# Plain blocks for the first weight tile, and partial sums kept in PSUM, in the feed-forward stage of an encoder kernel on one Trainium2 core

## The chip, the cores and the metric

The kernel runs on one core of one Trainium2 chip. The time is the device time of one execution in microseconds (us); the median of three runs of the kernel before is 2502.7 us, with runs from 2497.94 to 2503.45 us. The engines are TensorE (PE, with its weight loads as PEld), VectorE (DVE), ScalarE (ACT), GpSimd (POOL) and SyncE (SP), whose queue issues all transfers between HBM and the on-chip memory. "Granted clock" is the share of full speed that TensorE was allowed.

## The reference, cut to what matters

Two requests of 1024 tokens, each 1024 wide, go through one encoder layer with shared weights. The part that matters here is the feed-forward network behind attention:

```python
FFN_HIDDEN = -(-8 * D_MODEL // (3 * 256)) * 256      # 2816
...
xn = rms_norm(h, norm_ffn_g[l])
g, u = jnp.split(xn @ w_gate_up[l], 2, axis=-1)
h = h + (jax.nn.silu(g) * u) @ w_down[l]
h = rms_norm(h, final_norm_g)
```

Everything is float32. The kernel splits each float32 operand into a high and a low part of a reduced type (fp32r) and forms one product from three matmuls (high by high, high by low, low by high; `mm3`).

## The kernel before

The program treats request 0 and then request 1; each passes projection, attention and feed-forward. The feed-forward stage is written for Strassen's method in Winograd's form: a 2 by 2 block product in seven block products instead of eight. The products are called P1 to P7, and their operands are blocks or sums of blocks.

**Gate and up.** The input of this stage, 1024 tokens by 1024, is cut into four blocks: B11 and B21 are the two halves of the width for the even tiles of 128 tokens, B12 and B22 those for the odd tiles. The seven products need B11, B21 and B22 and the sums T1 to T4 of blocks, each transposed. `x_side` is a generator that makes these 28 pieces (seven operands by four tiles): VectorE or GpSimd forms the sums from the normalised rows `x2n`, TensorE transposes 128 by 128 pieces (`x_trans`, four transposes into one PSUM bank, tile name `tp`), ScalarE copies the high part out, and VectorE takes the remainder as the low part (`xB`, `xT`, `xT1l`, `xH` in the profile; sums in tile `t`). It runs beside the end of attention's output projection, and the rest of it is stepped between the matmuls of the first two weight tiles. There are 22 weight tiles of 128 gate and 128 up columns. `gu_unit(p, t)` computes one product of one tile: 4 steps of depth with 3 matmuls of 512 columns each, 12 matmuls; 84 for a tile. `prep_gu` makes the weight operand of a product, up to six operand tiles ahead (`prep`, ring `wop`). The result of a tile (`act`) goes to HBM as `ad`.

**Down.** The activations are read back (`a_load`, blocks `A[i, j, c]`, i for even or odd tokens, j for even or odd weight tile, c from 0 to 10), and the residual `h` is read back from `hd`. A product has 11 blocks c of 12 matmuls, 132 in all, 924 for the seven. `DN` gives the order of the products: P1, P2, P4, P5, P7, P6, P3. Each product has its own four PSUM banks, and when it is complete VectorE adds its banks onto `h` once for every output block that contains it (`C`, `add`, list `adds`), spread over the matmuls of the next product: 14 output blocks by 4 banks, 56 additions for a request. `prep_dn` forms the sums of activations and of weight rows and makes the high parts, `prep_dn_lo` the low ones (VectorE for the weights, GpSimd for the activations). They run ahead of TensorE by at most three blocks. The rows of `w_down` come in two ways: `trun` holds the first 512 columns of the even rows for the whole stage, and `wraw` is a ring of four tiles, each loaded in the order of the list `items` when the tile four places earlier has been freed (`load`, set `freed`).

**The order on SyncE's queue.** All transfers are issued by SyncE in the order of the program text. Behind the last product of the last weight tile, `gu_hook` issues the burst of loads that the down stage needs: the rest of `trun`, the rest of the activations of the early products, `h` (8 transfers of 512 KB), and the activations A[2, 2] (`aC`, `aB`) and A[2, 1] (`aD`, `aB`, `aS`). The core of it:

```python
elif p == "P3":
    for c in (6, 8, 10):
        T.trun_tile(c)
    ...
    for t_ in range(TT):
        sync.dma_start(out=h[:, t_, :], in_=T.hd[:, t_, :])
    a_load(2, 2, 0, hold["C"], 0, 8)
```

The main loop calls, for unit n, first `T.prep_ops(n)` (which also makes the low parts up to unit n + 1 and calls `load`), then the matmuls of the unit, then `gu_hook`. The low part of block 1 of the first down product is made in the call for the first down unit, so behind the burst in the program text.

## Time and profile before

| what | us |
|---|---|
| median of three runs | 2502.7 |
| the profiled execution | 2502.41 |
| its span, first to last instruction | 2500.6 |
| TensorE busy in it | 2357.3 (94%) |
| VectorE busy in it | 1790.1 (72%) |
| GpSimd busy in it | 1262.2 (50%) |
| ScalarE busy in it | 1188.8 (48%) |

The span is 1.8 us shorter than the profiled time. Busy time of TensorE is modelled from the start of pipelined matmuls, so a stage in which matmuls start late one after another can still read as busy; the count of matmuls in a stretch of known length says more. All rows of the kernel read L118, since one helper records every operation; operations are told apart by their tiles.

### The profile page before, as it was taken

To read this page: it belongs to the slowest core of one execution; us is meant where nothing else is said; L and a number is where in the kernel's file an instruction comes from. 1 tells how busy PE (TensorE), PEld (TensorE's weight loads), DVE (VectorE), ACT (ScalarE), POOL (GpSimd) and SP (SyncE) were. 2 spreads that over 40 slices of the span, in tenths; PEclk is the share of its full clock that TensorE was granted. 3 is DMA by queue.
4 is the path that set the end of the run, shared out by engine and by line. 5 is a ranking of instruction groups with operands and counts; after the bars stand their busy time and mean duration, and the time that the engine had idled before them with its cause. 6 is when DMAs were issued, how large, how long until landed. Compare 5 with 4: busy or idle time off the path is not lost. (4 is left out here: it accounts for less than half of the span.)

```text
span 2500.6 us, 34045 instructions
## 1 busy us (share of the span) xinstructions
PE 2357.3 (94%) x12402; PEld 1992.9 (80%) x12402; DVE 1790.1 (72%) x2480; ACT 1188.8 (48%) x2131; POOL 1262.2 (50%) x1156
## 2 busy tenths in 40 slices
PE   7998999988999999999988989999799999999997
PEld 7887899877888888777777789988678888887765
DVE  6686888876555555599966778888765555556996
ACT  4476667654232222343545776666542223224434
POOL 5323766644444444465663157665444444444665
PEclk9999999998999999999999989999999999999999
DMA  5113000111223222842430130001122222237413
GB/s 140 39 36 103 18 18 18 43 68 43 85 77 92 76 77 93 328 151 76 144 129 22 36 103 26 10 18 43 68 68 76 76 85 83 86 123 298 168 48 114
DMA packets 189704, 212.78 MB, mean 85 GB/s; under 512 B 24272, under 2 KB 141008, under 8 KB 188512
## 3 DMA queue, kind: packets, MB, share of 16 engines
q1 hardware_dynamic: 189536, 210.60, 25.8%
q8 instruction: 98, 1.61, 0.3%
q14 instruction: 70, 0.57, 0.1%
HBM read 168.45 MB, written 39.85 MB: 83 GB/s over the span
## 5 line engine op out<-in xcount | busy, mean ns | idle before, releaser
L118 PE MATMUL dn<-wop 128*128 128x512 f32 x1848 | 449.6, 401 | 18.3 <-DVE wop L118 14.7
L118 PEld LDWEIGHTS dn<-wop 128*128 128x128 f32 x1848 | 343.5, 189 | 117.6 <-DVE wop L118 36.9
L118 PE MATMUL gu<-xT,wop 128*128 128x512 f32 x1408 | 371.3, 394 | 0.0
L118 POOL TENSOR_TENSOR pexp<-pexp,rsum 128x1024 f32<-128x1024 f32 x128 | 242.9, 1898 | 228.7 <-DVE rsum L118 148.5
L118 POOL TENSOR_TENSOR wop<-wraw,wop 128x512 fp32r<-128x512 f32 x176 | 230.6, 1311 | 217.5 <-ACT wop L118 217.5
L118 PEld LDWEIGHTS gu<-xT,wop 128*128 128x128 f32 x1408 | 264.2, 188 | 59.2
L118 POOL TENSOR_TENSOR wop<-wsum,wop 128x512 fp32r<-128x512 f32 x132 | 171.7, 1301 | 266.9 <-ACT wop L118 266.9
L118 PE MATMUL gu<-xB,wop 128*128 128x512 f32 x1056 | 265.1, 398 | 3.0 <-DVE xB L118 3.0
L118 ACT CAST wop<-wraw 128x512 fp32r<-128x512 f32 x264 | 162.6, 616 | 215.4 <-DVE wraw L118 134.2
L118 PE MATMUL gu<-xH,wop 128*128 128x512 f32 x1056 | 254.7, 397 | 1.7 <-DVE act L118 1.7
L118 PEld LDWEIGHTS gu<-xH,wop 128*128 128x128 f32 x1056 | 198.8, 188 | 50.3 <-issue 2.5
L118 PEld LDWEIGHTS gu<-xB,wop 128*128 128x128 f32 x1056 | 199.3, 190 | 48.8 <-DVE xB L118 3.6
L118 ACT CAST pt<-ptp 128x512 fp32r<-128x512 f32 x256 | 148.9, 586 | 120.1 <-PE ptp L118 118.9
L118 DVE TENSOR_REDUCE m<-S 128x1 f32<-128x1041 f32 x128 | 158.1, 1235 | 55.6 <-PE S L118 54.8
L118 ACT ACTIVATE pexp<-S,m 128x1041 f32<-128x1041 f32 x128 | 145.1, 1133 | 66.9 <-DVE m L118 60.0
L118 DVE TENSOR_TENSOR pt<-ptp,pt 128x512 fp32r<-128x512 f32 x256 | 168.2, 681 | 5.4 <-ACT pt L118 4.4
L118 PE MATMUL ptp<-idf,pexp 128*128 128x128 f32 x1024 | 156.4, 277 | 10.2 <-DVE pt L118 6.7
L118 PE MATMUL pvo<-pt,vst 128*128 128x256 f32 x1024 | 156.5, 297 | 2.9 <-DVE attnT L118 2.9
L118 PE MATMUL S<-kh,qs 128*128 128x348 f32 (+1 forms) x384 | 136.9, 359 | 21.3 <-ACT pexp L118 14.9
L118 ACT CAST wop<-wsum 128x512 fp32r<-128x512 f32 x132 | 81.8, 620 | 141.9 <-DVE wsum L118 141.9
L118 DVE SCALAR_TENSOR_TENSOR act<-th,act 128x512 f32<-128x512 f32 x88 | 143.7, 1633 | 3.0
L118 PEld LDWEIGHTS ptp<-idf,pexp 128*128 128x128 f32 x1024 | 125.9, 143 | 21.3 <-issue 7.8
(289 smaller groups left out, 5189.2 us busy)
## 6 DMA issues: line engine op xcount, KB each, us to landing
wraw<-in_w_gate_up SPq DMA_DIRECT2D x176, 256.0 KB, 3.6
wraw<-in_w_down SPq DMA_DIRECT2D x110, 256.0 KB, 2.9
ad<-act SPq DMA_DIRECT2D x44, 512.0 KB, 3.5
wraw<-in_w_down SPq DMA_DIRECT2D x22, 512.0 KB, 3.3
wraw<-in_w_in SPq DMA_DIRECT2D x32, 256.0 KB, 3.4
hd<-h SPq DMA_DIRECT2D x16, 512.0 KB, 5.0
h<-hd SPq DMA_DIRECT2D x16, 512.0 KB, 10.3
out<-h SPq DMA_DIRECT2D x15, 512.0 KB, 2.6
```

Of the source, the lines that this page charges most:

```text
L118: return fn(*args, **kw)
```

## The change

- **First weight tile of gate and up.** Tile 0 is no longer computed by the seven products but by the eight plain block products (`FIRST`, `gu_first`): four weight blocks, each against two token blocks, 96 matmuls, added up in four PSUM banks. The transposed blocks that it needs are B11, B12, B21, B22; B12 is a new operand of `x_side`. The sums T2, T3 and T4 and their transposes are made between the matmuls of tile 0, and T1 last, in the buffers that B12 had.
- **Order of the down products.** It becomes P2, P1, P4, P6, P5, P7, P3. P6 and P7 go on adding in the banks of P1, and P3 in those of P5 (`onto`), so that an output block is added to `h` from a bank that holds several products. 8 output blocks by 4 banks are left, 32 additions for a request.
- **Preparation of the down operands.** The sums of activations are others. P1 and P7 get weight rows of their own through the ring (`two("P1", 1, L0)`, `two("P7", 0, L0)`), 22 transfers of 256 KB more for a request, and the additions that alternated between VectorE and GpSimd are all on VectorE.
- **Loads.** A[1, 2] takes the places and the times of A[1, 1] and the other way round. The burst of `gu_hook` is otherwise the same.

```diff
 GU = (("P1", "B11"), ("P6", "T2"), ("P2", "B21"), ("P7", "T3"), ("P5", "T1"), ("P4", "T4"), ("P3", "B22"))
-DN = ("P1", "P2", "P4", "P5", "P7", "P6", "P3")
+
+FIRST = {"A11": ("B11", "B12"), "A21": ("B11", "B12"), "A12": ("B21", "B22"), "A22": ("B21", "B22")}
+DN = ("P2", "P1", "P4", "P6", "P5", "P7", "P3")
...
         def x_side():
-            t23 = {}
-
             def blocks(q):
                 e, o = x2[2 * q], x2[2 * q + 1]
                 return e[:, :512], e[:, 512:], o[:, :512], o[:, 512:]
 
-            def sums(q, eng):
-                b11, b21, b12, b22 = blocks(q)
-                t23[q] = slot((S_CH, S_CL, "s6", "s2")[q], [P, 2, 512], name="t23")
-                dve.tensor_tensor(t23[q][:, 1], b22, b12, ALU.subtract)
-                eng.tensor_tensor(t23[q][:, 0], t23[q][:, 1], b11, ALU.add)
-                dve.tensor_tensor(b12, b12, b11, ALU.subtract)
-
-            def t4(q, eng):
-                b21 = blocks(q)[1]
-                eng.tensor_tensor(b21, t23[q][:, 0], b21, ALU.subtract)
+            def t1_place(name):
+                hi = slot("V", [P, 4, 512], F32R, name="x" + name)
+                X[name] = (hi, [(2 * i, slot(t, [P, 2, 512], F32R, name=f"x{name}l"))
+                                for i, t in enumerate(("s7", f"wl{b}"))])
 
             x_alloc("B11", T.xb[:1])
-            x_alloc("T2", T.xb[1:])
             for q in range(3):
                 while not {2 * q, 2 * q + 1} <= T.x2_done:
                     yield False
-                sums(q, (dve, pool, pool)[q])
-                yield True
                 x_trans("B11", q, blocks(q)[0])
-                yield True
-                x_trans("T2", q, t23[q][:, 0])
                 yield True
             while not T.out_done:
                 yield False
             x_alloc("B21", T.xa[:1])
-            x_alloc("T3", T.xa[1:])
-            hi = slot("V", [P, 4, 512], F32R, name="xT1")
-            X["T1"] = (hi, [(2 * i, slot(t, [P, 2, 512], F32R, name="xT1l")) for i, t in enumerate(("s7", f"wl{b}"))])
+            t1_place("B12")
             for q in range(3):
-                x_trans("T3", q, t23[q][:, 1])
+                x_trans("B12", q, blocks(q)[2])
                 yield True
                 x_trans("B21", q, blocks(q)[1])
-                t4(q, pool)
                 yield True
             while not {6, 7} <= T.x2_done:
                 yield False
-            sums(3, dve)
             x_trans("B11", 3, blocks(3)[0])
-            x_trans("T2", 3, t23[3][:, 0])
-            x_trans("B21", 3, blocks(3)[1])
-            t4(3, dve)
+            x_trans("B12", 3, blocks(3)[2])
             T.x_go = True
             yield True
-            x_trans("T3", 3, t23[3][:, 1])
+            x_trans("B21", 3, blocks(3)[1])
             yield True
-            for q in range(4):
-                x_trans("T1", q, blocks(q)[2])
-                yield True
+            x_alloc("T2", T.xb[1:])
+            x_alloc("T3", T.xa[1:])
             hx = slot("H", [P, 2, 2, 4, 512], F32R, name="xH")
             x_alloc("T4", (), both=hx[:, 0])
             x_alloc("B22", (), both=hx[:, 1])
             for q in range(4):
-                x_trans("T4", q, blocks(q)[1])
+                x_trans("B22", q, blocks(q)[3])
                 yield True
             for q in range(4):
-                x_trans("B22", q, blocks(q)[3])
+                b11, b21, b12, b22 = blocks(q)
+                t23 = slot(("s6", "s2")[q % 2], [P, 2, 512], name="t23")
+                dve.tensor_tensor(t23[:, 1], b22, b12, ALU.subtract)
+                dve.tensor_tensor(t23[:, 0], t23[:, 1], b11, ALU.add)
+                yield True
+                pool.tensor_tensor(b21, t23[:, 0], b21, ALU.subtract)
+                pool.tensor_tensor(b12, b12, b11, ALU.subtract)
+                x_trans("T2", q, t23[:, 0])
+                yield True
+                x_trans("T3", q, t23[:, 1])
+                yield True
+                x_trans("T4", q, b21)
+                yield True
+            while not T.b12_free:
+                yield False
+            t1_place("T1")
+            for q in range(4):
+                x_trans("T1", q, blocks(q)[2])
                 yield True
 
...
-        T.units = [("gu", p, t) for t in range(NHT) for p, _ in GU] + [("dn", p, c) for p in DN for c in range(NC)]
+        T.units = [("gu", p, 0) for p in FIRST] + [("gu", p, t) for t in range(1, NHT) for p, _ in GU] + [("dn", p, c) for p in DN for c in range(NC)]
...
         two("P2", 1, L0)
+        two("P1", 1, L0)
         for c in range(NC):
             items.append((("P4", c), [P, 2, 512], [(lambda r, i=i: r[:, i], rows(2 * c + i, L1)) for i in range(2)]))
+        two("P6", 0, L0)
         for c in range(NC):
             items.append((("P5", c), [P, 2, 512], [(lambda r: r.rearrange("p a b -> p (a b)"), rows(2 * c, slice(0, D)))]))
-        two("P6", 0, L0)
+        two("P7", 0, L0)
         two("P3", 1, L1)
...
         def prep_dn(p, c):
             tr = trun[c // 2][:, c % 2]
-            turn = (dve, pool)[c % 2]
-            if p == "P1":
+            r = raws[(p, c if p in ("P4", "P5") else c - c % 2)]
+            rc = r[:, c % 2]
+            if p == "P2":
+                src, s = rc, A[1, 2, c]
+            elif p == "P1":
                 src, s = tr, A[1, 1, c]
-            elif p == "P2":
-                src, s = raws[(p, c - c % 2)][:, c % 2], A[1, 2, c]
-                dve.tensor_tensor(tr, tr, src, ALU.subtract)
+                dve.tensor_tensor(A[2, 1, c], A[2, 1, c], A[2, 2, c], ALU.add)
             elif p == "P4":
-                r = raws[(p, c)]
                 b12, b22 = r[:, 0], r[:, 1]
                 dve.tensor_tensor(b22, b22, b12, ALU.subtract)
-                turn.tensor_tensor(b12, b22, tr, ALU.add)
+                dve.tensor_tensor(b12, b22, tr, ALU.add)
                 src, s = b12, A[2, 2, c]
+            elif p == "P6":
+                dve.tensor_tensor(A[1, 1, c], A[2, 1, c], A[1, 1, c], ALU.subtract)
+                dve.tensor_tensor(tr, tr, rc, ALU.add)
+                src, s = tr, A[1, 1, c]
             elif p == "P5":
-                r = raws[(p, c)]
-                dve.tensor_tensor(A[2, 2, c], A[2, 1, c], A[2, 2, c], ALU.add)
                 dve.tensor_tensor(r[:, 0], r[:, 1], r[:, 0], ALU.subtract)
-                src, s = r[:, 0], A[2, 2, c]
+                dve.tensor_tensor(A[2, 2, c], A[2, 2, c], A[1, 1, c], ALU.subtract)
+                src, s = r[:, 0], A[2, 1, c]
             elif p == "P7":
-                dve.tensor_tensor(A[2, 1, c], A[1, 1, c], A[2, 1, c], ALU.subtract)
-                src, s = tr, A[2, 1, c]
-                dve.tensor_tensor(A[1, 1, c], A[2, 2, c], A[1, 1, c], ALU.subtract)
-            elif p == "P6":
-                r = raws[(p, c - c % 2)]
-                dve.tensor_tensor(tr, tr, r[:, c % 2], ALU.add)
-                src, s = tr, A[1, 1, c]
+                dve.tensor_tensor(rc, tr, rc, ALU.subtract)
+                dve.tensor_tensor(A[1, 1, c], A[1, 2, c], A[1, 1, c], ALU.subtract)
+                src, s = rc, A[2, 2, c]
             else:
-                src, s = raws[(p, c - c % 2)][:, c % 2], A[1, 2, c]
+                src, s = rc, A[1, 1, c]
             sop, top = op_tile(), op_tile()
             act.copy(sop[:, 0], s)
             act.copy(top[:, 0], src)
             if p == "P4":
                 act.copy(tr, r[:, 1])
-            if p == "P6":
-                turn.tensor_tensor(A[1, 2, c], A[1, 2, c], A[1, 1, c], ALU.subtract)
             half[p, c] = src, s, sop, top
 
         def prep_dn_lo(p, c):
@@ -1757,11 +1756,12 @@
             dve.tensor_tensor(top[:, 1], src, fv(top[:, 0]), ALU.subtract)
             pool.tensor_tensor(sop[:, 1], s, fv(sop[:, 0]), ALU.subtract)
             ops["dn", p, c] = (q4((sop[:, 0], sop[:, 1])), (top[:, 0], top[:, 1]))
-            if p in ("P2", "P6", "P3"):
-                if c % 2 or c == NC - 1:
-                    freed.add((p, c - c % 2))
-            elif p in ("P4", "P5"):
+            if p == "P1":
+                dve.tensor_tensor(src, src, raws[(p, c - c % 2)][:, c % 2], ALU.subtract)
+            if p in ("P4", "P5"):
                 freed.add((p, c))
+            elif c % 2 or c == NC - 1:
+                freed.add((p, c - c % 2))
 
...
+        def gu_first(p):
+            n = tuple(FIRST).index(p)
+            if n == 0:
+                st_t[0] = Trunk()
+                st_t[0].bk = [bank(0, i, "gu") for i in range(4)]
+            v = st_t[0]
+            wh, wl = ops.pop(("gu", p, 0))
+            for half, xn in enumerate(FIRST[p]):
+                need(xn, 4)
+                xh, xls = T.X[xn]
+                bk = v.bk[2 * half + n % 2]
+                for k in range(4):
+                    k0, xl = next((k0, x) for k0, x in xls if k0 <= k < k0 + x.shape[1])
+                    mm3(bk, wh[:, k], wl[:, k], xh[:, k], xl[:, k - k0], n < 2 and k == 0, n >= 2 and k == 3)
+                    next(side, None)
+                if n == 2 and half == 0:
+                    v.a = slot("s5", [P, 2, 512], name="act")
+                if n == 2:
+                    act.activation(v.a[:, half], bk, AF.Tanh, scale=0.5)
+                    dve.scalar_tensor_tensor(v.a[:, half], v.a[:, half], 1.0, bk, ALU.add, ALU.mult)
+                elif n == 3:
+                    dve.scalar_tensor_tensor(v.a[:, half], v.a[:, half], 0.5, bk, ALU.mult, ALU.mult)
+            if n == 1:
+                T.b12_free = True
+            if n == 3:
+                sync.dma_start(out=T.ad[:, :, 0, 0, :], in_=v.a)
...
-                a_load(1, 1, 0, slot(xb[0], [P, 8, 512], name="aA"), 0, 8)
+                a_load(1, 2, 0, slot(xb[0], [P, 8, 512], name="aA"), 0, 8)
...
-                a_load(1, 1, 10, hold["B"], 2, 1)
+                a_load(1, 2, 10, hold["B"], 2, 1)
                 k4, s5 = (slot(x, [P, 2, 512], name="aS") for x in (S_K, "s5"))
-                a_load(1, 2, 4, k4, 0, 2)
-                a_load(1, 2, 6, s5, 0, 1)
-                a_load(1, 2, 7, hold["V"], 0, 4)
+                a_load(1, 1, 4, k4, 0, 2)
+                a_load(1, 1, 6, s5, 0, 1)
+                a_load(1, 1, 7, hold["V"], 0, 4)
...
-        C = {"P1": ((1, 1, 1), (1, 2, 1), (2, 1, 1), (2, 2, 1)), "P2": ((1, 1, 1),), "P3": ((1, 2, 1),),
-             "P4": ((2, 1, -1),), "P5": ((1, 2, 1), (2, 2, 1)), "P6": ((1, 2, 1), (2, 1, 1), (2, 2, 1)),
-             "P7": ((2, 1, 1), (2, 2, 1))}
+        C = {"P2": ((1, 1, 1),), "P1": ((1, 1, 1),), "P4": ((2, 1, -1),), "P6": ((1, 2, 1),), "P5": ((2, 2, 1),),
+             "P7": ((2, 1, 1), (2, 2, 1)), "P3": ((1, 2, 1),)}
+        onto = ("P6", "P7", "P3")
...
-                banks[n] = [bank(n % 2, q, "dn") for q in range(4)]
+                banks[n] = banks[n - 2] if p in onto else [bank(n % 2, q, "dn") for q in range(4)]
             (sh, sl), (th, tl) = ops.pop(("dn", p, c))
             due = -(-len(adds) // (NC - c)) if p != "P3" else min(2, len(adds))
             for q in range(4):
-                mm3(banks[n][q], sh[:, q], sl[:, q], th, tl, c == 0, c == NC - 1)
+                mm3(banks[n][q], sh[:, q], sl[:, q], th, tl, c == 0 and p not in onto, c == NC - 1, p in onto)
...
-        guards = {("gu", "P5", 0): ("T4", 1), ("gu", "P4", 0): ("B22", 1), ("gu", "P3", 0): ("B22", 2)}
+        guards = {("gu", "P1", 1): ("T4", 1), ("gu", "P6", 1): ("T1", 1), ("gu", "P2", 1): ("T1", 2)}
...
-            if kind == "gu":
+            if p in FIRST:
+                gu_first(p)
+            elif kind == "gu":
```

## Rows read from the trace of the kernel before

**Rows 1.** Page, first line: span and number of instructions.

```profile
span 2500.6 us, 34045 instructions
```

**Rows 2.** Timeline of PE, request 0's turn to gate/up: start, us, instructions [idle before, releaser].

```profile
562.63 1.12 PE L118 MATMUL tp<-idf,t 128*128 128x128 f32 x4 [5.91 <-POOL t L118]
...
567.90 1.97 PE L118 MATMUL tp<-idf,t 128*128 128x128 f32 x8 [3.30 <-POOL t L118]
...
576.97 1.05 PE L118 MATMUL tp<-idf,t 128*128 128x128 f32 x4 [2.21 <-DVE t L118]
...
580.27 1.65 PE L118 MATMUL gu<-xB,wop 128*128 128x512 f32 x3 [1.40 <-DVE xB L118]
...
608.36 2.92 PE L118 MATMUL gu<-xB,wop 128*128 128x512 f32 x12
```

**Rows 3.** Groups of DVE from 549.6 to 580.3 us: count, busy us, mean ns, idle before.

```profile
L118 DVE SCALAR_TENSOR_TENSOR x2n<-h,rs,gffn 128x1024 f32<-128x1024 f32 x7 | 8.9, 1279 | 2.9 <-POOL rs L118 2.9
L118 DVE TENSOR_TENSOR xB<-tp,xB 128x512 fp32r<-128x512 f32 x8 | 5.5, 686 | 0.4 <-ACT xB L118 0.3
L118 DVE TENSOR_TENSOR xT<-tp,xT 128x512 fp32r<-128x512 f32 x7 | 4.7, 686 | 1.2 <-ACT xT L118 1.2
L118 DVE TENSOR_TENSOR x2n<-x2n 128x512 f32<-128x512 f32 x4 | 2.8, 689 | 0.1
L118 DVE TENSOR_TENSOR t<-x2n 128x512 f32<-128x512 f32 x4 | 2.7, 684 | 0.0
```

**Rows 4.** Window of 10 us before request 0's gate/up: length, busy by engine, granted clock, DMA.

```profile
560.00:570.00 10.00, 4.07 (x18) 3.67 (x19) 7.01 (x11) 3.00 (x6) 5.01 (x6) 0.50 0.13 52
```

**Rows 5.** Timeline of PE at the start of the down stage, both requests.

```profile
1023.44 71.52 PE L118 MATMUL dn<-wop 128*128 128x512 f32 x301 [2.57 <-DVE wop L118]
...
2255.40 3.18 PE L118 MATMUL dn<-wop 128*128 128x512 f32 x13
2261.12 70.07 PE L118 MATMUL dn<-wop 128*128 128x512 f32 x301 [2.54 <-DVE wop L118]
```

**Rows 6.** Windows, second request, down products P2, P4, P5, P7, P6: PE, PEld, DVE, ACT, POOL busy (count), clock, DMA.

```profile
2288.82:2319.41 30.59, 30.59 (x134) 24.83 (x132) 27.32 (x38) 13.61 (x24) 15.08 (x11) 1.00 0.55 208
2319.41:2352.33 32.92, 31.43 (x133) 24.59 (x132) 32.78 (x33) 16.74 (x30) 23.77 (x15) 1.00 0.48 160
2352.33:2384.21 31.88, 31.88 (x134) 24.06 (x132) 31.81 (x38) 13.43 (x23) 16.57 (x12) 1.00 0.54 181
2384.21:2419.59 35.38, 33.34 (x133) 24.00 (x132) 35.07 (x41) 13.08 (x24) 22.88 (x14) 1.00 0.01 2
2419.59:2455.58 35.99, 32.46 (x134) 24.15 (x133) 34.67 (x37) 12.79 (x23) 22.36 (x16) 1.00 0.23 82
```

**Rows 7.** Tile views: VectorE sums with a bank as input, and with two on-chip tiles (ns min/median/max).

```profile
L118 DVE TENSOR_TENSOR h<-h,dn x112: 670/679/684, 1051.4 to 2488.3; 128x512 f32<-128x512 f32 x112
...
L118 DVE TENSOR_TENSOR aC<-aD,aC x16: 1174/1482/1791, 1110.3 to 2366.8; 128x512 f32<-128x512 f32 x16
```

**Rows 8.** Timeline of SP: the burst of request 1, and the first weight rows behind each burst.

```profile
1051.51 0.81 SPq L95 DMA_DIRECT2D wraw<-in_w_down  x2
...
2265.11 8.54 SPq L95 DMA_DIRECT2D h<-hd  x8
...
2280.84 0.32 SPq L95 DMA_DIRECT2D aS<-ad  x1
2287.65 0.81 SPq L95 DMA_DIRECT2D wraw<-in_w_down  x2
```

**Rows 9.** Transfers issued from 1051 to 1052.2, and from 2287 to 2289: median us to landing.

```profile
wraw<-in_w_down SPq DMA_DIRECT2D x2, 256.0 KB, 9.1
...
wraw<-in_w_down SPq DMA_DIRECT2D x2, 256.0 KB, 11.4
```

**Rows 10.** Page, transfers of the whole run: median us to landing.

```profile
wraw<-in_w_down SPq DMA_DIRECT2D x110, 256.0 KB, 2.9
```

**Rows 11.** Page, costliest groups: the copy of a weight operand's high part on ACT.

```profile
L118 ACT CAST wop<-wraw 128x512 fp32r<-128x512 f32 x264 | 162.6, 616 | 215.4 <-DVE wraw L118 134.2
```

More of the change, by code (lines that the diff above doesn't have):

```diff
@@ L1457, in attention @@
         X = T.X = {}
-        T.x_in = {n: 0 for _, n in GU}
+        T.x_in = {n: 0 for n in ("B12", *(n for _, n in GU))}
+        T.b12_free = False
         T.x_mk = bank_t
@@ L1696, in prep_gu @@
                 dve.tensor_tensor(sums[t][:, 1], a12, sums[t][:, 1], ALU.subtract)
-            src = {"P1": a11, "P2": a12, "P4": a22, "P7": a21}.get(p)
+            src = {"P1": a11, "P2": a12, "P4": a22, "P7": a21, "A11": a11, "A21": a21, "A12": a12, "A22": a22}.get(p)
             if src is None:
@@ L1700, in prep_gu @@
             ops[("gu", p, t)] = split(src, pool, 4)
-            if p == "P7":
+            if p in ("P7", "A21"):
                 freed.add((t, 0))
-            if p == "P3":
+            if p in ("P3", "A22"):
                 freed.add((t, 1))
@@ L1793, in prep @@
             lows(n + 2)
-        T.before_prep = lambda u: u[1:] == ("P1", 0)
+        T.before_prep = lambda u: u[1:] == ("A11", 0)
         load()
@@ L1823, in gu_post @@
             elif p == "P2":
-                if t == 0:
+                if t == 1:
                     need("T4", 2)
@@ L1832, in gu_post @@
             elif p == "P5":
-                if t == 0:
-                    need("B22", 3)
+                if t == 1:
+                    need("T4", 4)
                 v.a = slot((S_XIN, S_GW)[t % 2], [P, 2, 512], name="act")
@@ L1853, in gu_unit @@
                 v.bk = {}
+                if t == 1:
+                    need("T4", 3)
                 pu = slot(("s6", S_GR)[t % 2], [P, 2, 512], name="p1u2")
@@ L1867, in gu_unit @@
                 mm3(bk, wh[:, k], wl[:, k], xh[:, k], xl[:, k - k0], first and k == 0, k == 3, not first)
-                if t < 2 and k < 3:
+                if t == 1 and k < 3:
                     next(side, None)
             gu_post(p, t, bk)
+        def gu_first(p):
[24 more added lines that the diff above has]
+                sync.dma_start(out=T.ad[:, :, 0, 0, :], in_=v.a)
         xa, xb = T.xa, T.xb
@@ L1893, in gu_hook @@
                 hold["B"] = slot(xb[1], [P, 8, 512], name="aB")
-                a_load(1, 1, 8, hold["B"], 0, 2)
+                a_load(1, 2, 8, hold["B"], 0, 2)
             elif p == "P2":
@@ L1903, in gu_hook @@
                 hold["V"] = v4
-                a_load(1, 2, 0, w, 0, 2)
-                a_load(1, 2, 2, s7, 0, 2)
+                a_load(1, 1, 0, w, 0, 2)
+                a_load(1, 1, 2, s7, 0, 2)
             elif p == "P3":
@@ L2031, in before_prep @@
                     return False
-            if u[0] == "dn" and u[1] == "P1":
-                return (1, 1, u[2]) in A
+            if u[0] == "dn" and u[1] == "P2":
+                return (1, 2, u[2]) in A
             if nxt is not None and u[0] == "dn":
-                if u[1:] == ("P6", NC - 3):
+                if u[1:] == ("P7", NC - 3):
                     T.no_rope = True
@@ L2053, in ffn @@
             cur[0] = n
-            if n == len(GU):
+            if n == len(FIRST) + 5:
                 for _ in side:
```

## Prediction

> **What bounds the kernel now.** I read the page first for the span [rows 1], and then four stretches: the turn from attention to gate/up, the first weight tile, the start of the down stage and its seven products. Between them, in the tiles of gate and up, TensorE runs without a gap and the change touches nothing.
>
> At the turn, TensorE's timeline shows it short of operands: before the first gate/up matmul it stands idle 5.91, 3.30, 2.21 and 1.40 us, 12.8 in all, and the releasers are the tile `t`, the sums of blocks, and a last low part [rows 2]. The reader should see whose work is late: VectorE makes 15 low parts and 11 sums in this stretch (eight of them in the two largest groups) and waits 2.9 us for GpSimd, which is busy with sums of its own when the row scales of the last norms are wanted [rows 3]. In such a stretch the granted clock is 0.50, the lower of its two levels (1.2 GHz), with TensorE 4.07 of 10 us busy [rows 4].
>
> In the down stage the windows by product show the limit moving. P2 takes 30.59 us for its 132 matmuls with VectorE 27.32 us busy: TensorE's pace. P4, P5, P7 and P6 take 32.92, 31.88, 35.38 and 35.99 us with VectorE busy in nearly all of it: VectorE's pace [rows 6]. A block of 12 matmuls at full pace is 12 x 70.07 / 301 = 2.79 us [rows 5].
>
> The last view is SyncE's queue with its landings. Behind the last gate/up product stands the burst: `h` is issued from 2265.11, and the last activations at 2280.84. The first weight rows behind it are issued at 2287.65 and take 11.4 us to land, where such a transfer takes 2.9 us over the whole run [rows 8 to 10]. In request 0 they are issued at 1051.51 and take 9.1 us. So the queue is clear at about 2299.0 and 1060.6. Today nobody waits for these rows: they belong to block 8 of P2, the second product.
>
> **The change part by part.** Durations are of the profiled execution, 2502.4 us, 0.3 us under the median of the three runs.
>
> *Start of gate/up.* Before the first matmul VectorE loses 4 of its 15 low parts (T2 and T3 give way to B12, and one B21 moves behind): 4 x 0.686 = 2.7 us. It loses all 11 sums, at 0.687 from the two groups 7.6 us, and the 2.9 us of waiting for GpSimd, whose sums go too [rows 3]. That is 13.2 us; TensorE's idle time there is 12.8 [rows 2]. What is late next is the last norm, whose chain stays, so I take 12.5 for the earlier start. If GpSimd's waiting only changes its name, it is 9.8.
>
> *First weight tile.* It ran from 580.27 to 608.36, 28.1 us [rows 2]: 84 matmuls at 0.2328 are 19.6 us, and the other 8.5 us fall on the 13 groups of transposes between them, slow clock included, 0.66 each. Then: 96 matmuls are 22.3 us, and 21 groups (32 with B12's four, less the 11 before the start) are 13.8 us. That is 36.1. New are the sums between matmuls. For each token tile, the two sums stand on VectorE behind the low part of the group before: copy 0.62 [rows 11], low part 0.69, two sums 1.37, together 2.7 us, while TensorE has six matmuls, 1.4 us. So 0 to 1.3 us of wait, four times; half of it, 2.6, is taken. 38.7 against 28.1 is +10.6. With the earlier start the turn gives -1.9 for a request, -3.8 for two, and bounds of -4.5 (no new wait) to +3.4 (the full wait, 9.8 gained) for each. The two operations behind the last product of the tile go; they were beside the next tile's matmuls and cost nothing either way.
>
> *Down: work of VectorE.* The additions from PSUM fall from 56 to 32 for a request, 24 x 0.679 = 16.3 us [rows 7]. The sums of two on-chip tiles rise from 89 to 110 (before: P2 11, P4 and P6 17, P5 and P7 22; then 22 in each of P1, P4, P6, P5 and P7), and GpSimd's 10 go. What matters is the load of a product: P1, P4, P6, P5 and P7 each get 33 operations of this kind (22 sums, 11 low parts) and 4 additions, P2 only its 11 low parts, and P3 these and 8 additions. Exactly 33 and 4 is P5 of the kernel before: 31.88 us [rows 6]. Five of these are 159.4 us, where P2, P4, P5, P7 and P6 took 166.8: -7.4 for a request, -14.7 for two. Bounds: at P2's pace -13.8 for each, and 0 if the five stay at their old mean.
>
> Rows 7 show what speaks against this part: a sum of two on-chip tiles takes 1.17 to 1.79 us, an addition with a PSUM bank 0.67 to 0.68 each time. The Trainium skill (SBUF — State Buffer, Who interferes with whom) has the rule: an operation of VectorE with two SBUF inputs shuts out, or waits for, GpSimd's reads, one with a single SBUF input doesn't. The change trades the second kind for the first. By that rule alone, every new sum at the 1.48 of rows 7, the trade would be 21 x 1.48 - 16.3 = +14.8 for a request. The sum here goes by P5's row, where GpSimd runs its one operation for each block beside the 33.
>
> *Down: the wait that the order adds.* P2 is now first. Its weight rows come through the ring of four tiles of two blocks, so blocks 0 to 7 are there before the burst, and the rows of blocks 8 and 9 can be issued only when block 1's low part is made. That happens in the call for the first down unit, which the program has behind `gu_hook`. On SyncE's in-order queue they stand behind the last activations (2280.84 [rows 8]), and on the transfer engines behind the burst itself. So block 8's rows land when the queue is clear, at 2299.0 and 1060.6. Then come ScalarE's copy (0.62) and VectorE's low part (0.69): 2300.3 and 1061.9.
>
> TensorE is there sooner. In request 1 it has done 13 matmuls at 2261.12, after the wait of 2.54 behind the last gate/up result, which stays; block 8 is 83 matmuls on, 2280.4. In request 0: 1023.44 + 19.3, and 1.45 for the slower start of that stretch (71.52 against 70.07 us for 301 matmuls) is 1044.2 [rows 5]. The waits are 19.9 and 17.7 us, 37.6 together. Behind block 8 wait blocks 9 and 10, and on VectorE the first sums of P1, whose activations A[2, 1] are ahead in the same queue and so cost nothing more. The lower bound is a landing that the burst doesn't hold up: 2280.84 + 0.32 + 2.9 = 2284.1, a wait of 5.0 us; the upper one is the value taken. I take the upper, since the row that I use is the transfer itself.
>
> After such a wait TensorE may come back at the lower clock. The 1.45 us above is what a wait of 2.57 cost in request 0; in request 1 the like wait cost nothing. I take 1.45 for each request, 2.9, with 0 and two blocks at half speed (5.6 each) as bounds.
>
> *At nothing.* The 22 additional transfers for each request (5.6 MB) go into products where the transfer engines are 0.01 to 0.55 busy [rows 6]; uncovered, one costs its 2.9 us. The exchange of A[1, 1] and A[1, 2] moves the same bytes. The last product begins with 8 additions instead of 12, so the next request's transposes start two blocks sooner: at most 5.6 us once, taken as nothing, since the work behind them has its own chain.
>
> **Sum.** 2502.4 - 3.8 + 37.6 + 2.9 - 14.7 = 2524.4; predicted 2524 us.
>
> **The rivals.**
> - *The rows of block 8 are there in time* (the other side). For it: the four ring tiles are freed early, and a transfer of this size needs only 2.9 us [rows 10]. Against it: 11.4 and 9.1 us just behind the burst [rows 9]. With waits of at most 5.0 us: 2502.4 - 3.8 - 14.7 + 0 to 10 = 2484 to 2494, say 2489. It decides from landings 11 us sooner in each request on (22 us over time before, by two). The Trainium skill (DMA: Bandwidth & Descriptors, Two DMAs through the same engine are not ordered) states that nothing orders transfers across the 16 engines; by that the small transfer could pass the large ones. The rows above show it waiting. Chance 0.10.
> - *VectorE isn't relieved.* The wait comes, and 21 sums at P5's mean, (31.81 - 4 x 0.68) / 33 = 0.88, against 24 additions at 0.679 leave it +2.2 for each request instead of -7.4: 2544. For it: 99% busy in four products [rows 6]. Against it: GpSimd's ten sums go, and P5 shows the new load's time. Chance 0.07.
> - *The first tile eats more*: full waits, 9.8 gained: +3.4 instead of -1.9 for each request, 2535. Chance 0.05.
> - *The change pays its own wait*: the down products at TensorE's pace (-27.6) and the turn at -9: 2503 to 2506, within 0.2%. Chance 0.04.
> - The forecast has 0.74.
>
> **Range and chances.** 0.2% (5 us) is about what a measurement of this kernel can tell from no change. Faster 0.10 (first rival), same 0.04 (fourth), slower 0.86. The bounds of the down work and of the clock alone give 2508 to 2544 around the forecast; that takes in the second and third rival and leaves out the first, so the range is 2508 to 2545.
>
> **What would show it.** In the profile after: a gap of 15 to 20 us on TensorE inside the first down product of each request, after some 96 matmuls, released by the low part of `wraw`, with SyncE having issued that pair at about the end of the burst; the first gate/up matmul some 12 us sooner than 580.27, and the first tile some 38 us long; 64 additions `h<-h,dn` instead of 112; down products from the second on at about 31.9 us. The prediction is wrong if the pair lands before TensorE reaches block 8, or if a product with 33 sums runs far from 31.9 us.

## The result, and the profile after

The kernel after takes 2524.99 us (median of four runs, 2521.34 to 2526.87), beside 2500.32 us for the kernel before on the same chip: 1.0101 times, with a 95% interval of 1.0085 to 1.0118. The profiled execution took 2523.67 us, its span is 2521.6. From the page: the span, the engines' busy time, and the group of the down matmuls with the idle time of TensorE ahead of it and what ended most of it.

```profile
span 2521.6 us, 34189 instructions
...
PE 2354.6 (93%) x12458; PEld 1995.9 (79%) x12458; DVE 1774.0 (70%) x2466; ACT 1184.6 (47%) x2131; POOL 1221.9 (48%) x1136
...
L120 PE MATMUL dn<-wop 128*128 128x512 f32 x1848 | 449.2, 401 | 56.1 <-ACT wop L120 36.7
```

VectorE is busy 16.1 us less than before, GpSimd 40.3 us less, and the span is 21.0 us longer [rows 1]. The time stands in the last line: of TensorE's 56.1 us of waiting ahead of down matmuls, 36.7 end with a copy of ScalarE. By the medians the change costs 24.7 us, by the two profiled executions 21.0; what follows takes these 21.0 apart. TensorE's timeline at the start of both down stages shows that these are two waits (start, us, matmuls in a row, idle time before and its releaser):

```profile
1009.68 3.19 PE L120 MATMUL dn<-wop 128*128 128x512 f32 x13
1015.39 19.46 PE L120 MATMUL dn<-wop 128*128 128x512 f32 x83 [2.52 <-DVE wop L120]
1052.69 36.64 PE L120 MATMUL dn<-wop 128*128 128x512 f32 x145 [17.84 <-ACT wop L120]
...
2264.08 19.53 PE L120 MATMUL dn<-wop 128*128 128x512 f32 x83 [2.52 <-DVE wop L120]
2302.43 42.22 PE L120 MATMUL dn<-wop 128*128 128x512 f32 x169 [18.82 <-ACT wop L120]
```

13 + 83 = 96 matmuls are blocks 0 to 7: the wait stands exactly ahead of block 8, where [rows 5] had 301 matmuls without a gap. The queue of SyncE says why: the rows of block 8 (the first of the three `wraw`) are issued behind the whole burst.

```profile
2269.95 7.46 SPq L97 DMA_DIRECT2D h<-hd  x8
...
2283.51 0.32 SPq L97 DMA_DIRECT2D aS<-ad  x1
2284.84 2.86 SPq L97 DMA_DIRECT2D wraw<-in_w_down  x3
```

In request 0 the same two, alone in their window, with the time to landing in the last column: the weight rows take 16.8 us, as long as the activations just ahead of them, against 2.9 for such a transfer over the run before [rows 10].

```profile
aS<-ad SPq DMA_DIRECT2D x1, 256.0 KB, 17.5
wraw<-in_w_down SPq DMA_DIRECT2D x1, 256.0 KB, 16.8
```

Behind the landing come the copy and the low part, in one row each of ScalarE and VectorE; the copy's idle time ends with the transfer, and TensorE starts at 2302.43, with the copy's end and beside the low part:

```profile
2301.76 0.62 ACT L120 CAST wop<-wraw 128x512 fp32r<-128x512 f32 x1 [25.28 <-DMA wraw<-in_w_down]
```

```profile
2302.41 0.69 DVE L120 TENSOR_TENSOR wop<-wraw,wop 128x512 fp32r<-128x512 f32 x1 [25.73 <-ACT wop L120]
```

Block 8 itself is slow. In its window (columns as in [rows 6]) the granted clock is 0.50, the lower of its two levels (1.2 GHz), and its 12 matmuls take 5.59 us; block 9, with 0.96, takes 2.92.

```profile
1052.69:1058.28 5.59, 5.59 (x13) 4.10 (x14) 5.24 (x4) 2.55 (x5) 4.67 (x3) 0.50 0.68 248
```

At the turn of request 0, TensorE's timeline answers to [rows 2]: the first gate/up matmul at 562.57 instead of 580.27, and four waits inside the tile, which ends at 601.02.

```profile
557.23 2.82 PE L120 MATMUL tp<-idf,x2n 128*128 128x128 f32 x12 [2.66 <-DVE xB L120]
560.44 1.89 PE L120 MATMUL tp<-idf,x2n 128*128 128x128 f32 x12 [0.39 <-DVE xB12l L120]
562.57 1.24 PE L120 MATMUL gu<-xB,wop 128*128 128x512 f32 x3 [0.24 <-DVE xB L120]
...
571.62 0.63 PE L120 MATMUL tp<-idf,t 128*128 128x128 f32 x4 [1.42 <-DVE t L120]
...
601.02 2.90 PE L120 MATMUL gu<-xB,wop 128*128 128x512 f32 x12
```

Not all of these 17.7 us are the change's. The eight matmuls into tile `spa`, late in attention, have 3337 matmuls ahead of them in request 0, the same ones in the same order in both kernels (the other engines' instructions are the same ones up to there too), and yet they start 3.0 us sooner after the change. So the turn is measured from `spa`, here in the kernel before and the kernel after, request 0 and then request 1:

```profile
544.98 1.05 PE L118 MATMUL spa<-ones,attnT 128*128 128x2 f32 x8 [0.60 <-DVE attnT L118]
541.94 1.05 PE L120 MATMUL spa<-ones,attnT 128*128 128x2 f32 x8 [0.60 <-DVE attnT L120]
...
1783.35 1.05 PE L118 MATMUL spa<-ones,attnT 128*128 128x2 f32 x8 [0.60 <-DVE attnT L118]
1790.08 1.05 PE L120 MATMUL spa<-ones,attnT 128*128 128x2 f32 x8 [0.59 <-DVE attnT L120]
```

The five middle products of request 1, P1, P4, P6, P5, P7, in windows with the columns of [rows 6]:

```profile
2313.51:2344.26 30.75, 30.75 (x133) 24.73 (x132) 30.37 (x35) 11.95 (x21) 15.48 (x11) 1.00 0.26 86
2344.26:2378.84 34.58, 32.33 (x134) 24.29 (x132) 34.27 (x40) 18.59 (x33) 17.71 (x11) 1.00 0.53 175
2378.84:2412.35 33.51, 31.24 (x134) 24.59 (x132) 33.51 (x39) 14.00 (x23) 18.68 (x13) 1.00 0.27 87
2412.35:2445.23 32.88, 31.54 (x133) 24.54 (x132) 32.88 (x38) 12.57 (x22) 16.30 (x12) 1.00 0.55 175
2445.23:2477.53 32.30, 31.22 (x133) 24.58 (x132) 29.34 (x35) 12.57 (x22) 17.23 (x12) 1.00 0.27 93
```

They add up to 164.0 us, where five products of [rows 6] took 166.8; VectorE still fills four of the five. So the 21 us, stage by stage from the two traces (starts of `spa` and of down in each request):

| stretch | before | after | difference |
|---|---|---|---|
| to `spa` of request 0, same matmuls in the same order | 545.0 | 541.9 | -3.0 |
| from there to request 0's down | 472.8 | 467.7 | -5.0 |
| request 0's down | 241.5 | 259.9 | +18.4 (wait and slow blocks +20.8, the rest -2.4) |
| to `spa` of request 1, in another order | 524.1 | 520.5 | -3.7 |
| from there to request 1's down | 472.1 | 468.3 | -3.8 |
| request 1's down | 230.9 | 250.8 | +19.8 (wait and slow blocks +21.7, the rest -1.9) |
| behind it | 14.3 | 12.5 | -1.8 |

### The profile page after: what moved, and what is told of

It reads as the page before. It is cut to its first block, busy times and chain, and to the rows that moved or that the text cites. A ratio compares the mean times of both kernels' runs of the same rounds, so it can differ in the third digit from the quotient of the medians.

```text
span 2521.6 us, 34189 instructions
## 1 busy us (share of the span) xinstructions
PE 2354.6 (93%) x12458; PEld 1995.9 (79%) x12458; DVE 1774.0 (70%) x2466; ACT 1184.6 (47%) x2131; POOL 1221.9 (48%) x1136
## 4 chain that ended last, share of the span: by engine, by line
PE 59%; DVE 22%; ACT 7%; issue 4%; DMA 4%; POOL 3%; SPq 1%; DVEq 0%; POOLq 0%; ACTq 0%
PE gu L120 34%; PE op L120 6%; PE S L120 4%; PE pvo L120 4%; PE ptp L120 4%; DVE wop L120 3%; ACT arena L120 3%; DVE wraw L120 2%; PE dn L120 2%; DVE arena L120 2%; DVE h L120 1%; DMA wraw<-in_w_down 1%; DVE aS L120 1%; PE qp L120 1%; PE pin L120 1%
## 5 line engine op out<-in xcount | busy, mean ns | idle before, releaser
L120 PE MATMUL dn<-wop 128*128 128x512 f32 x1848 | 449.2, 401 | 56.1 <-ACT wop L120 36.7
L120 PE MATMUL gu<-xT,wop 128*128 128x512 f32 x1344 | 352.0, 394 | 0.0
L120 ACT CAST wop<-wraw 128x512 fp32r<-128x512 f32 x286 | 175.8, 617 | 320.8 <-DVE wraw L120 225.5
L120 PEld LDWEIGHTS gu<-xT,wop 128*128 128x128 f32 x1344 | 252.7, 188 | 57.9
L120 PE MATMUL gu<-xB,wop 128*128 128x512 f32 x1136 | 288.4, 397 | 0.3 <-DVE xB L120 0.2
L120 POOL TENSOR_TENSOR wop<-wsum,wop 128x512 fp32r<-128x512 f32 x126 | 163.0, 1294 | 256.2 <-ACT wop L120 256.2
L120 PEld LDWEIGHTS gu<-xB,wop 128*128 128x128 f32 x1136 | 212.4, 189 | 47.7 <-DVE xB L120 0.8
L120 DVE TENSOR_TENSOR wop<-wraw,wop 128x512 fp32r<-128x512 f32 x110 | 99.2, 906 | 80.4 <-ACT wop L120 80.4
## 6 DMA issues: line engine op xcount, KB each, us to landing
h<-hd SPq DMA_DIRECT2D x16, 512.0 KB, 10.3
```

The source lines that it names most:

```text
L120: return fn(*args, **kw)
```

## The experiments

Each ratio is to the kernel before, run on the same chip, with its 95% interval.

**The wait: order in the queue or bytes?** In `e1_burst_late` the part of the burst from `h` on is issued after block 2 of P2, behind the rows of blocks 8 to 10:

```diff
-                h = T.h = slot("H", [P, TT, D], name="h")
-                ...
-                a_load(2, 1, 10, s5, 1, 1)
+        def dn_hook(p, c):          # called behind each dn_unit
+            if (p, c) != ("P2", 2):
+                return
+            ...                     # the same loads
```

> Changed kernel, but the loads of h, A[2, 2] and A[2, 1] are issued behind block 2 of P2 instead of behind the last gate/up product, so that all weight rows of P2 stand ahead of them in the queue. Theory (the order in the queue makes the wait): block 8 no longer waits; what is late next is A[2, 1], which VectorE needs for the first sum of P1 and behind which it has the low part of block 10; it should land some 42 us after the start of the down stage, so block 10 waits some 13 us in each request instead of block 8's 18 to 19, and the time falls by about 12 us to 2513. Rival 1 (the bytes of the burst have to land first, in whatever order): the wait keeps its length, 2525. Rival 2 (the wait only uses up time that VectorE or the first tile would lose anyway): no gap of over 5 us, but the time stays at 2520 to 2525.

Measured 2514.62 us, 1.0062 (1.0044 to 1.0079), as expected. All rows of P2 are now ahead of the burst, and block 8 doesn't wait. Block 10 does, behind its first matmul (13 + 108 matmuls are blocks 0 to 9 and one more), by 12.16 us, in request 1 by 11.43:

```profile
1013.11 25.27 PE L120 MATMUL dn<-wop 128*128 128x512 f32 x108 [2.53 <-DVE wop L120]
1050.54 36.19 PE L120 MATMUL dn<-wop 128*128 128x512 f32 x144 [12.16 <-DVE wop L120]
```

What is late is A[2, 1] (`aD`), which is in the burst. VectorE's first sum of P1 waits for it, and the low part of block 10 stands behind that sum in VectorE's order:

```profile
1049.19 0.69 DVE L120 TENSOR_TENSOR aD<-aD,aC 128x512 f32<-128x512 f32 x1 [18.00 <-DMA aD<-ad]
1049.80 0.68 DVE L120 TENSOR_TENSOR wop<-wraw,wop 128x512 fp32r<-128x512 f32 x1
```

`e2_burst_by_need` moves the same bytes, each load where it is first needed: half of A[2, 2], A[2, 1] and `h` in `gu_hook`, the others after blocks 0, 2, 4, 6 and 8 of P2, weight rows between them.

```diff
+                a_load(2, 2, 0, hold["C"], 0, 4)
+                a_load(2, 1, 0, hold["D"], 0, 4)
-                for t_ in range(TT):
+                for t_ in range(0, TT, 2):
                     sync.dma_start(out=h[:, t_, :], in_=T.hd[:, t_, :])
...
+        def dn_hook(p, c):
+            ...
+            elif c == 4:
+                a_load(2, 1, 4, hold["D"], 4, 4)
+                T.trun_tile(6)
```

> Changed kernel, with the same loads as before but issued in the order in which they are needed: first half of A[2, 2] and A[2, 1] and the even tiles of h behind the last gate/up product, the rest of A[1, 1], A[2, 2], A[2, 1] and trun spread over blocks 0 to 6 of P2, the odd tiles of h behind block 8. Theory (order in the queue): both waits and the slow clock behind them go, 20.8 us in request 0 and 21.7 in request 1, so 2525 - 42 = 2483, some 17 below the kernel before. Rival 1 (the bytes are the limit): a wait of over 10 us stays somewhere in P2 or P1, and the time is above 2505. Rival 2 (the loss lies in VectorE's sums and the first tile): the waits go, the time stays above 2515.

Measured 2487.53 us, 0.9958 (0.9943 to 0.9973). No block of P2 behind the start waits:

```profile
1009.31 3.18 PE L120 MATMUL dn<-wop 128*128 128x512 f32 x13
1015.03 35.19 PE L120 MATMUL dn<-wop 128*128 128x512 f32 x151 [2.53 <-DVE wop L120]
```

Some 37 us lie between the two orders of the same transfers. The loss of the change is the order of its loads in the queue: block 8's rows behind the burst.

**The first tile alone.** `e3_first_tile` is the kernel before with the first part of the change: `FIRST`, `gu_first` and the new `x_side`; the down stage is the old one.

```diff
+FIRST = {"A11": ("B11", "B12"), "A21": ("B11", "B12"), "A12": ("B21", "B22"), "A22": ("B21", "B22")}
 DN = ("P1", "P2", "P4", "P5", "P7", "P6", "P3")
```

> Kernel before with the first part of the change alone: plain blocks for the first weight tile, the down products in their old order with their old loads and additions. By the trace of the changed kernel the turn and the first tile give 8 us in request 0; theory: 2 x 8 = 16 below the kernel before, 2484 to 2486. Rival (the earlier start is given back in the tile by 12 more matmuls, 8 more groups of transposes and the new waits for sums, as I had put it in the prediction): 2 to 4 us, 2496 to 2499.

Measured 2488.65 us, 0.9954 (0.9938 to 0.9971). Down starts at 1010.21 and 2241.26 instead of 1017.73 and 2255.40. From `spa` it is 467.7 and 468.6 us to the start of down, against 472.8 and 472.1 before: the first tile gives 5.1 and 3.5 us, some 8.5 of the 10.9 by which the kernel is faster. So the time lies between the two that were expected: the 8 us of request 0, on which the theory stood, held 3.0 from ahead of the turn. `e2` with both parts is not measurably faster than this part alone: the new order of the products brings little.

**The waits in the tile.** `e4_sums_ahead` is `e2` with the sums of a token tile formed one tile ahead, between the T2 and T3 transposes of the tile before:

```diff
             for q in range(4):
-                ...
-                x_trans("T2", q, t23[:, 0])
+                x_trans("T2", q, t23s[q][:, 0])
                 yield True
-                x_trans("T3", q, t23[:, 1])
+                if q < 3:
+                    sums(q + 1)
+                x_trans("T3", q, t23s[q][:, 1])
```

> As e2_burst_by_need, and in the first weight tile the sums for a token tile are made one step earlier: those of tile 0 before the last transposes of B22, those of tile q + 1 between the transposes of T2 and T3 of tile q. Theory: the four waits of 1.42 us for each request before the transposes of T2 are the latency of VectorE's queue and go; 11 us less than e2_burst_by_need, about 2472. Rival (VectorE is short of time in this tile, so that the wait comes back at T3, T4 or T1): the same time as e2_burst_by_need within 3 us.

Measured 2484.74 us, 0.9940 (0.9924 to 0.9955): 2.8 us under `e2`, within the noise, where 11 were expected. The tile takes 35.62 us instead of 38.45, with waits of 0.99, 0.33, 1.30 and 0.29 left. VectorE and GpSimd in the tile show what goes with the last three: GpSimd's sums now run beside VectorE's, and one of these takes 1.18 us. No run takes GpSimd's sums out of this tile, so that they cause these 1.9 us is argued from the durations.

```profile
569.46 1.18 DVE L120 TENSOR_TENSOR t<-x2n 128x512 f32<-128x512 f32 x1
570.68 0.69 DVE L120 TENSOR_TENSOR t<-t,x2n 128x512 f32<-128x512 f32 x1
```

```profile
568.81 1.29 POOL L120 TENSOR_TENSOR x2n<-x2n 128x512 f32<-128x512 f32 x1
```

**What holds VectorE in the down products?** `e5_no_gpsimd_low` is `e4` without GpSimd's one operation for a block; ScalarE writes a copy in the place of the activations' low part, so this part of the computation is changed.

```diff
-            pool.tensor_tensor(sop[:, 1], s, fv(sop[:, 0]), ALU.subtract)
+            act.copy(sop[:, 1], s)
```

> As e4_sums_ahead, but in the down stage GpSimd does not form the low part of the activations; ScalarE writes a rounded copy of the activations in its place (the computation is changed there: the low part is wrong, the matmuls and their number are the same). VectorE keeps all its operations. Theory (VectorE's 33 operations on two on-chip tiles for each of the products P1, P4, P6, P5, P7 are held up by GpSimd's one operation a block, about 1.1 us each time): without it VectorE needs 3 x 0.6 us and an addition now and then, under TensorE's 2.79 a block; the five products fall from 165 to 166 us to 153 to 155, and the time by 22 to 25 to about 2461. Rival (the number of VectorE's operations, or the chain sum, copy, low part, sets the pace): the five products keep 160 us or more, and the time falls by less than 10.

Measured 2447.07 us, 0.9798 (0.9782 to 0.9813). All five products fall to TensorE's pace, 30.50 to 30.62 us in both requests. Two of the windows (P1, P4 of request 1):

```profile
2247.82:2278.39 30.57, 30.57 (x133) 24.80 (x132) 24.67 (x41) 19.34 (x35) 0.00 (x0) 1.00 0.83 308
2278.39:2308.99 30.60, 30.60 (x134) 24.79 (x132) 24.40 (x40) 22.99 (x42) 0.00 (x0) 1.00 0.58 196
```

VectorE's own operations are unchanged in number. Its groups over the five products of request 1, first in the kernel after, then here (count, busy us, mean ns):

```profile
L120 DVE TENSOR_TENSOR wop<-wraw,wop 128x512 fp32r<-128x512 f32 x35 | 29.3, 839 | 2.9 <-ACT wop L120 2.9
L120 DVE TENSOR_TENSOR wraw<-wraw 128x512 f32<-128x512 f32 x22 | 22.5, 1023 | 0.0
...
L120 DVE TENSOR_TENSOR h<-h,dn 128x512 f32<-128x512 f32 x22 | 14.8, 676 | 0.0
...
L120 DVE TENSOR_TENSOR aS<-aD,aS 128x512 f32<-128x512 f32 x7 | 10.1, 1441 | 0.0
```

```profile
L120 DVE TENSOR_TENSOR wop<-wraw,wop 128x512 fp32r<-128x512 f32 x35 | 24.2, 692 | 24.0 <-ACT wop L120 24.0
L120 DVE TENSOR_TENSOR wraw<-wraw 128x512 f32<-128x512 f32 x22 | 15.1, 685 | 0.2 <-DMA wraw<-in_w_down 0.2
L120 DVE TENSOR_TENSOR h<-h,dn 128x512 f32<-128x512 f32 x22 | 14.9, 681 | 0.0
...
L120 DVE TENSOR_TENSOR aS<-aD,aS 128x512 f32<-128x512 f32 x7 | 4.8, 685 | 0.0
```

Every group of three or more with two on-chip tiles falls to 0.69 us, from 0.84 to 1.44; the addition with a PSUM bank is 0.68 either way. VectorE had no idle time because GpSimd stretched its operations. This agrees with the rule of the Trainium skill (SBUF — State Buffer, Who interferes with whom) that stands in the prediction. Against `e4` the five products give 12.6 us for each request, 25.2 of the 35.1 us between the two spans; P2 and P3 give 5.7, and 4.2 lie in the stretch between the two down stages, of which below.

`e6_p4_turns` goes the other way: `e4` with one of P4's sums in every second block given to GpSimd.

```diff
-                dve.tensor_tensor(b12, b22, tr, ALU.add)
+                (dve, pool)[c % 2].tensor_tensor(b12, b22, tr, ALU.add)
```

> As e4_sums_ahead, but in P4 the second sum of weights goes to GpSimd in every odd block, as in the kernel before. Theory (each GpSimd operation shuts VectorE out for about as long as the VectorE operation that it saves takes, and more): P4 stays between 33 and 35 us, the time within 3 us of e4_sums_ahead. Rival (VectorE has too many operations): P4 falls from 34.5 to 32.9 us or below, and P4 was the product in which the change lost by moving this sum.

Measured 2488.17 us, 0.9960 (0.9946 to 0.9974). P4 of request 1, in `e4` and here:

```profile
2301.63:2336.14 34.51, 32.35 (x133) 24.26 (x132) 34.20 (x40) 18.60 (x33) 17.72 (x11) 1.00 0.53 175
```

```profile
2305.44:2340.99 35.55, 31.96 (x134) 24.41 (x132) 35.41 (x33) 17.87 (x33) 26.48 (x17) 1.00 0.49 161
```

VectorE has seven operations fewer in the window, and it is busy 1.2 us longer: here taking work off VectorE by giving it to GpSimd makes the product slower.

**The best version, and what its lead is worth.** `e7_sums_first` moves the sums of `e4` one step further ahead, `e8_old_down` gives the same first tile to the old down stage (`e3`).

```diff
-                if q == 2:
+                if q == 1:
                     sums(0)
...
             for q in range(4):
-                x_trans("T2", q, t23s[q][:, 0])
-                yield True
                 if q < 3:
                     sums(q + 1)
+                x_trans("T2", q, t23s[q][:, 0])
+                yield True
```

> As e4_sums_ahead, but in the first weight tile VectorE gets the sums of token tile q + 1 ahead of the low part of T2 of tile q, one step sooner still. Theory (the rest of the waits before T2, 2.9 us for each request, is VectorE's queue: sums behind a low part that waits for ScalarE): they go to below 1 us, the tile from 35.6 to 33 us, 4 to 6 us less than e4_sums_ahead. Rival (GpSimd's sums hold VectorE's up, whenever they come): the tile stays above 35 us, the time within 2 us.

> e3_first_tile (kernel before, first part of the change alone) with the sums as in e7_sums_first. It tells what the new order of the down products is worth when nothing waits for weight rows: e7_sums_first against it. My prediction had 14.7 us in favour of the new order; by the five products of e2_burst_by_need (165.9 and 165.7 us) against those of e3_first_tile (165.6 and 166.8) it is 0 to 1 us, so I expect this kernel within 3 us of e7_sums_first, 2478 to 2483.

Measured 2477.97 us, 0.9918 (0.9904 to 0.9932), for `e7`, and 2488.22 us, 0.9959 (0.9947 to 0.9972), for `e8`. Both expectations missed. The tile in `e7` is 35.31 and 34.73 us, not much shorter than the 35.62 and 36.33 of `e4`, and yet the kernel is 6.8 us faster (5.5 by the ratios). And `e8` is 10.3 us slower than `e7`, though request 0's down stage, from its first matmul to its last, takes 240.4 us in `e8` and 240.5 in `e7`. The two differ in the stretch from there to request 1's gate/up, 551.0 against 541.1 us: the same code, but the program's planner puts its instructions in another order when the work around it has other lengths. So the next four runs vary that alone: `pe.off` shifts the planner's time grid for TensorE from request 1 on, by 1.7 or 0.85 us.

```diff
...
     for b in range(2):
+        pe.off = 1.7 * b
         p1(trunks[b], b)
```

> e7_sums_first, with nothing changed but the planner's model: from request 1 on the grid of its clock model is shifted by 1.7 us, so that the program orders the work of request 1's projection and attention otherwise. In the profiles of e7_sums_first and e8_old_down that stage took 541.5 and 551.4 us with the same code, in another order of instructions. Theory (the 10 us between the two are the order that the planner happens to write, and no worth of the new down products): this kernel and e8_old_down's twin come out several us from their originals, in no fixed direction, and the difference of the pair isn't 10 us any more. Rival (the new order of the down products is worth 10 us, by work that it leaves to the next request): this one stays within 3 us of e7_sums_first, 2475 to 2481.

> e8_old_down with the same shift of 1.7 us in the planner's model from request 1 on. Theory: some us from e8_old_down's 2488, in either direction. Rival: within 3 us of e8_old_down, 2485 to 2491, and 10 us above e9_grid_new.

> e7_sums_first with a shift of 0.85 us instead: a second draw of the order for request 1. Theory: the time of request 1's projection and attention lies anywhere from 540 to 552 us; the total 2474 to 2488. Rival: within 3 us of e7_sums_first.

> e8_old_down with a shift of 0.85 us: a second draw for the old order of the down products. Theory: 2476 to 2490, so that the old and the new order of the products overlap. Rival: 2485 to 2491, above both draws of the new order.

| shift | new down order | old down order |
|---|---|---|
| none | `e7` 2477.97, 0.9918 | `e8` 2488.22, 0.9959 |
| 1.7 us | `e9` 2476.41, 0.9914 (0.9899 to 0.9928) | `e10` 2482.37, 0.9935 (0.9918 to 0.9951) |
| 0.85 us | `e11` 2482.68, 0.9935 (0.9918 to 0.9952) | `e12` 2480.98, 0.9930 (0.9915 to 0.9945) |

Only `e9` stayed within 3 us of its original. With nothing but the grid shifted, the times of a column differ by up to 6.3 and 7.2 us, and the two columns overlap; their means, 2479.0 and 2483.9, differ by less than the spread of either. Not all of that is the planner's order: up to `spa` of request 0 `e7`, `e9` and `e11` issue the same matmuls in the same order, and their profiled executions are there at 538.8, 543.4 and 544.1 us. `e9` and `e7` are the fastest: 19 to 23 us under the kernel before, and 47 to 49 under the change as it was made. By the times the new down order is worth 0 to 5 us. The traces narrow it: both down stages and what is behind the last add up to 484.3 to 484.7 us with the new order, and to 485.8 to 487.2 with the old, so 1 to 3 us, if the order costs the work beside it nothing.

## Why the prediction was right

The time, 2525.0 against 2524, and the mechanism that decides were right. That the two are 1 us apart is luck: two other terms were wrong and cancelled, and 6.7 us come from stretches that the change leaves as they are.

| term | predicted | measured |
|---|---|---|
| the turn and the first tile, two requests | -3.8 | -8.8 (-8.5 in `e3`) |
| ahead of `spa` in both requests | 0 | -6.7 |
| the wait ahead of block 8 | +37.6 | +37.0 (18.0 and 19.0) |
| slow blocks behind it | +2.9 | +5.5 |
| down work of VectorE | -14.7 | -4.2 |
| behind the last product | 0 | -1.8 |
| sum | +22.0 | +21.0 |

- *The wait* was priced by its place (96 matmuls) and its landing. Its releaser is the copy, not the low part, whose 0.69 us the price had too. The extra time of block 7, 20.80 - 2.79 and 21.78 - 2.79 us, is 37.0. That the queue's order makes it is shown by `e1` and `e2`. The first rival, landings in time, fell.
- *The slow blocks.* Block 8 took 5.59 and 5.51 us instead of 2.79, so +2.8 and +2.7: the step that took 1.45 from a wait of 2.57 us was too small for one of 18, and the upper bound of two blocks at half speed (5.6 each) too large. With that bound for each request and the down work at 0, the range's sum goes up to 2547, not 2544.
- *The turn.* The earlier start, taken as 12.5, was 14.7 and 12.8 us (from `spa` to the first gate/up matmul 20.6 and 21.2 us instead of 35.3 and 34.0); the 17.7 between 580.27 and 562.57 holds the 3.0 from ahead of `spa`. In request 0 TensorE's idle time fell by 9.5 (12.8 to 3.3). The other 5.2 is time of its own matmuls, which was not in the sum: four groups of four transposes fewer stand ahead of the start, and the granted clock was 0.83 in the 10 us before it, where [rows 4] has 0.50; how much each gives isn't shown. The tile, 38.45 and 39.01 us, fits the 38.7 predicted, but by two errors: all four waits came in full (4 x 1.42 = 5.7, not 2.6), and the 21 groups of transposes cost 10.4 instead of 13.8 us (38.45 - 22.3 - 5.7).
- *Ahead of `spa`.* Request 0 has the same matmuls in the same order there, and 3.0 us are within what profiled executions of the same order differ by (538.8 to 544.1 above); request 1's projection and attention have another order, and in the versions with this first tile they took 520 to 530 us from the last down matmul to `spa`. The 6.7 us are not the change's gain.
- *Down.* The step that failed is the price from P5's row, "Exactly 33 and 4 is P5 of the kernel before: 31.88 us". The five took 30.8 to 35.1, 164.8 and 164.0 in all, where 159.4 was predicted; by the prediction's own sign, a product with 33 sums far from 31.9 us, this part was wrong. A product's time here isn't set by the count of VectorE's operations, but by how far GpSimd's stretch them (`e5`, `e6`). The second rival was half right: VectorE was hardly relieved. The rule of the Trainium skill (SBUF — State Buffer, Who interferes with whom) that I weighed against the row had the mechanism, as `e5` shows; the sum of +14.8 by it was too far the other way, since the groups of sums take 0.99 to 1.44 us on average, not the 1.48 that [rows 7] have for one tile, and GpSimd's own sums went.

## What to carry to other kernels

When the order of consumers changes on a kernel whose loads share one queue, write down for each load what is first to need it, and reorder the queue as well: here the same bytes in two orders are 37 us apart. Price a VectorE operation with two on-chip inputs by what GpSimd does at that moment, and test it by taking GpSimd's operation away before moving work between the two. Where a planner orders instructions, a difference of some microseconds between two versions is a draw: shift the planner a little and measure several times before crediting an edit. And when two traces are compared, start from the last instruction that both reach by the same work: here 3 us of a seeming gain of 8 lay ahead of the change.

## What was not expected of the hardware

GpSimd's 11 operations, 1.4 to 1.6 us each on average, cost TensorE up to 4.5 us a product, though GpSimd is only half busy in it (17.7 of 34.6 us in P4): without them the five products take 152.7 us, 30.5 each, the pace of P2 before. And behind a wait of 18 us one block of 12 matmuls took twice as long (5.5 to 5.6 us, at a granted clock of 0.50), while the next took 2.79 or 2.92 us (at 1.00 and 0.96).
